# Output weights loaded into the difference buffers, a third PSUM bank for the heads' projections, and another order in the last attention block

## The chip, the cores and the metric

The kernel runs on one core of a Trainium2 chip. The metric is the device time of one execution in microseconds (us). PE is the matmul engine, DVE the vector engine, ACT the scalar (activation) engine, POOL the general-purpose engine, and SP the engine whose queue issues the DMAs here. SBUF is the on-chip working memory, PSUM the eight banks into which PE writes.

## The reference

One decoder layer on 1040 tokens (16 meta tokens and 1024 others) of width 1024. The part that matters here:

```python
a = rmsnorm(h, ln_mix_pre)
proj = a @ w_in
dq, dk, dv, hq, hf, hi, hg = split(proj)
y_diff = diff_attention(dq, dk, dv, ...)     # 4 heads: two softmaxes, p0 - lam * p1, times v, normalised
y_hgrn = hgrn2(hq, hf, hi, hg, ...)          # 4 heads: gated linear recurrence over the tokens
mix = concat([y_diff, y_hgrn]) @ w_out
h = h + rmsnorm(mix, ln_mix_post)
h = h + rmsnorm(conv_ffn(rmsnorm(h, ln_ffn_pre)), ln_ffn_post)
```

## The kernel before, in words

Tokens lie in nine blocks (one of 16 rows, eight of 128) and three groups of blocks, of 272, 384 and 384 columns (`GROUPS`). Matmuls are done on pairs of rounded operands: each value is split into a high and a low part (`split`, ACT makes the high part, DVE or POOL the rest), and three matmuls replace one.

**The order on PE is the program's.** PE follows the text of the program exactly; on the other engines a planner places the instructions by their readiness in its own estimate, except where `issue_after(x)` says that what is traced inside stands behind `x` on x's engine. SP's queue is worked off in the order in which the planner puts its DMAs, and so is every engine: an instruction that waits holds back all behind it.

**interleave (L61)** mixes two kinds of work on PE. `dense` yields projection or output matmuls one by one with a charged cost; the sides are heads, which yield a weight at each point where PE may be given other work. At such a point `fill * weight` units of dense matmuls follow (`FA, FH, FO = 840, 800, 800`). For a projection matmul the charge is `max(115, 0.42 * columns)` (L240), for an output matmul 216.

**Heads.** For each of four heads h, the projections of the HGRN head (hf, hq, hi, hg) run beside attention head h (L916), then those of the next attention head (dq, dk, dv) beside HGRN head h (L919). HGRN head 3 runs beside the first half of the output projection (L1071). `proj_group` (L231) makes one projection for one group of blocks in one PSUM tile from `ps_in`.

**PSUM** has three tags with two buffers each (L146 to L154): "ip" (projections, output sums), "m" (transposes, levels and others) and "S" (two banks per buffer: attention scores, and the HGRN head's output `po`).

**Attention (L624).** For a block, `scores` makes the two score matrices, finds the negative maximum on DVE, and ACT makes the exponentials. The last block has 1040 columns and needs a third bank E, so it has two maxima, and L673 takes the smaller of the two negated ones, `mx`, a DVE instruction on one column; ACT's two exponentials wait for it. At the end DVE combines both softmaxes in `pb` (one instruction over all columns). `values` (L685) transposes `pb` on PE in pieces of four blocks (`pt`) and copies each piece to `at`, in turn on DVE and ACT. `apply` (L710) multiplies by v into `pa`. The order on PE near the end is: scores of block 8 for the second softmax, values of block 7, apply of block 7, values of block 8, apply of block 8.

**HGRN (L413).** `diag`, then seven levels (L445): PE makes small products (`pl`) of the running q and k, then DVE multiplies parts of k (`kr`) and of q (in `mix`) by decays and copies the products to `am`. Each level's products need the multiplies of the level before. Each yields 3 (L503, L506). Level 2 also has POOL make further products of decays. Then three chains (L510), one per group: transposes of k (`pk`, copied to `kn`), `pu`, states `st`, the outputs `po`, their norm `on`, transposes `ss`.

**The difference buffers (L191 to L219).** `wd_sums` loads pieces of the FFN's down weights into five buffers (`wd`) of 256 KB, subtracts them on DVE, and stores the differences; it goes one step per projection group and is done before the last attention head ends. The pool `wdsums` stands on the left side of SBUF, between the activations and the attention pool, and closes with them (L923).

**The output stage (L944 to L1071).** `load_wr(n, k)` loads a 128 x 512 piece of the output weights, half n, k-th of eight, into one of three raw buffers ("wr"); `load_wo` splits it. First half: L1001 splits the mix of the first two blocks and stores the parts (`mix_split`, to `msc`, read back by `mix_load` for the second half), then L1003 loads and splits all eight pieces. `out_first` (L1034) sums the first half block by block; meanwhile two pieces of the second half are loaded ahead (L1045), and each block splits those loaded during the one before (L1047 to L1050).

Of the kernel before, what the change touches and what calls it, by code (L numbers as in the profile page):

```python
# [87 lines left out]
def layer_kernel(ctx: ExitStack, tc: tile.TileContext, x, meta, table, lbl, gpre, gpost, win,  # L88
# [99 lines left out]
        base = start(GROUPS[g][0])  # L188
        return acts[l][g][:, ks, t0 - base:t1 - base]

    ws_cm, wsp = pool("wdsums", 5)  # L191
    wsp.tile([P, 32], F32, tag="lineup_ws", name="lineup_ws", bufs=1)

    last_load = []

# [27 lines left out]

    wd_sums = down_sums()
    at_p_cm, ap_ = pool("attn", 1)
    z_cm, zp = pool("pre", 2, "right")

    def load_m(m, name, where=None, bufs=4):
        return [load_split(win[m][:, 512 * c: 512 * (c + 1)], f"{name}_{c}", where, bufs) for c in range(2)]

    def proj_group(g, parts, name, evac):  # L231
        b0, b1 = GROUPS[g]
        t0, t1 = start(b0), start(b1 - 1) + P
        n = t1 - t0
        pt = ps_in(f"pi_{name}_{g}")
        for k in range(KD):
            yield from proj_step(pt[:, :n], parts, k, t0, t1, lambda: evac(g, b0, b1, t0, t1, pt[:, :n]))

# [174 lines left out]
    def hgrn_head(t, done=None):  # L413
# [89 lines left out]
        yield 3  # L503
        for lev in range(1, 8):
            level(lev)
            yield 3  # L506

        states = {0: None}

# [114 lines left out]
    def attn(h, tens):  # L624
# [4 lines left out]
        def scores(i):  # L629
            r = rows(i)  # L630
            q0 = start(i)
            W = q0 + r
            nm = f"{h}_{i}"
            pb = ap_.tile([P, 2, L], F32, tag="pb", name=f"pb{nm}", bufs=2)
            st = ap_.tile([P, 12], F32, tag="st", name=f"ast{nm}", bufs=3)
            pend[i] = pb
            nearw = min(256, W)
            j0 = P if i == 0 else 256 - nearw

            def qk_mm(dst, m, c0, n):  # L640
                T.matmul(dst, qs[m][:, q0:q0 + P], ks[m][:, c0:c0 + n], start=True, stop=False)
                T.matmul(dst, qs[m][:, q0:q0 + P], kl[m][:, c0:c0 + n], start=False, stop=True)

            nmx, sm, rc = st[:r, 0:2], st[:r, 2:4], st[:r, 4:5]
            if W <= 512:
                S = ps_s(f"S{nm}")
                for m in range(2):
                    qk_mm(S[:, m, :W], m, 0, W)
                near = S[:r, :, W - nearw:W]
                V.tensor_tensor(near, near, rr[:r, j0:j0 + nearw].rearrange("p (o c) -> p o c", o=1).to_broadcast([r, 2, nearw]), op=ALU.add)  # L650
                V.tensor_reduce(nmx, S[:r, :, :W], axis=AX.X, op=ALU.max, negate=True)
                for m in range(2):
                    A.activation(pb[:r, m, :W], S[:r, m, :W], AF.Exp, bias=nmx[:, m:m + 1], accum_out=sm[:, m:m + 1])
            else:
                for m in range(2):
                    S = ps_s(f"S{nm}_{m}")
                    hw = (W if W <= 912 else 528) // 2
                    for p_ in range(2):
                        qk_mm(S[:, p_, :hw], m, p_ * hw, hw)
                    mx = nmx[:, m:m + 1]  # L660
                    if W <= 912:
                        near = S[:r, 1, hw - 256:hw]
                        V.tensor_tensor(near, near, rr[:r], op=ALU.add)
                        V.tensor_reduce(mx, S[:r, :, :hw], axis=AX.XY, op=ALU.max, negate=True)
                        A.activation(pb[:r, m, :W].rearrange("p (a c) -> p a c", a=2), S[:r, :, :hw], AF.Exp, bias=mx, accum_out=sm[:, m:m + 1])
                    else:
                        E = ps_m(f"E{nm}_{m}")
                        qk_mm(E, m, 528, 512)
                        V.tensor_tensor(E[:r, 256:], E[:r, 256:], rr[:r], op=ALU.add)
                        ex = st[:r, 6 + 2 * m:8 + 2 * m]  # L670
                        V.tensor_reduce(ex[:, 0:1], S[:r, :, :hw], axis=AX.XY, op=ALU.max, negate=True)
                        V.tensor_reduce(ex[:, 1:2], E[:r], axis=AX.X, op=ALU.max, negate=True)
                        V.tensor_tensor(mx, ex[:, 0:1], ex[:, 1:2], op=ALU.min)  # L673
                        A.activation(pb[:r, m, :528].rearrange("p (a c) -> p a c", a=2), S[:r, :, :hw], AF.Exp, bias=mx, accum_out=ex[:, 0:1])
                        A.activation(pb[:r, m, 528:W], E[:r], AF.Exp, bias=mx, accum_out=ex[:, 1:2])
                        V.tensor_tensor(sm[:, m:m + 1], ex[:, 0:1], ex[:, 1:2], op=ALU.add)
                    if m == 0:
                        yield 0.7
            V.reciprocal(rc, sm[:, 1:2])
            V.scalar_tensor_tensor(rc, sm[:, 0:1], nlam[:r], rc, ALU.mult, ALU.mult)  # L680
            V.scalar_tensor_tensor(pb[:r, 0, :W], pb[:r, 1, :W], rc, pb[:r, 0, :W], ALU.mult, ALU.add)
            pend["sum", i] = sm[:, 0:1]
            yield 1.3 if W <= 512 else 0.7

        def values(i):  # L685
# [7 lines left out]
            for pi, blks in enumerate(pieces):  # L693
# [8 lines left out]
                    A.copy(az[i % 2][:META, :r], pt[:META, :r])  # L702
                lo = 1 if pi == 0 else 0
                if n0 > lo:
                    (A.copy if pi % 2 else V.tensor_copy)(at[:, lo:n0], pv[:, lo:n0])
                ats.append(at)
                yield 0.8 if i < 4 else 0.6
            pend["ats"] = ats, pieces
# [44 lines left out]
                yield from values(i + 1)  # L753
        carry.append(pend.pop("tail"))

    def dense(tiles, preload=None, side=iter(())):
        parts = preload
        for idx, (m, name, evac) in enumerate(tiles):
            if parts is None:
                parts = load_m(m, name)  # L760
            nxt = load_m(tiles[idx + 1][0], tiles[idx + 1][1]) if idx + 1 < len(tiles) else None
            for g in range(3):
                next(side, None)
                for step, c in enumerate(proj_group(g, parts, name, evac)):
                    if step == 8:
                        flush()
                    yield c
            parts = nxt
# [145 lines left out]
    for h in range(HEADS):  # L914
        t_h, tiles_h = hgrn_in(h)
        interleave(dense(tiles_h, None, wd_sums), [attn(h, t_a)] + carried(), FA, 1500)  # L916
        if h < HEADS - 1:
            t_a, tiles_a = attn_in(h + 1)
            interleave(dense(tiles_a, None, wd_sums), [hgrn_head(t_h)] + carried(), FH, 1500)  # L919

    assert next(wd_sums, wd_sums) is wd_sums
    line_up(hp, 24)
    close(at_p_cm, ws_cm, at_cm)  # L923
    y_cm, yp = pool("y0", 1)
    y0 = yp.tile([P, NBLK, 512], F32, tag="y0", name="y0")
    m0 = yp.tile([P, KD, 36], F32R, tag="m0", name="m0")
# [15 lines left out]
    kept = kpp.tile([P, 2, KD, P], F32R, tag="kept", name="kept")  # L942

    def load_wr(n, k):  # L944
        raw = wp.tile([P, 512], F32, tag="wr", name=f"wor{n}_{k}", bufs=3)
        last_load.append(SY.dma_start(raw, wout[P * k: P * (k + 1), 512 * n: 512 * (n + 1)]))
        return n, k, raw

# [49 lines left out]
                T.matmul(py[:34], m0[:, k, :34], wo[k][l], start=(k == 0 and l == 0), stop=(k == last and l == 1))  # L998
                yield 216

    sps = [mix_split(i, 0, 4) for i in FIRST[:2]]  # L1001
    mix_split(0, 0, 7)
    wo0 = [load_wo(*load_wr(0, k)) for k in range(KD)]  # L1003
    wo = []

    pre_last = {}
# [27 lines left out]
    def out_first():  # L1034
# [5 lines left out]
        for j in range(2):  # L1040
# [1 line left out]
            if j == 0:  # L1042
                sp_ = mix_split(FIRST[2], 0, 4)
            A.copy(y0[:, FIRST[j]], pys[j])
        nxt = [load_wr(1, k) for k in (0, 1)]  # L1045
        for n, i in enumerate(FIRST[2:]):
            for w in nxt:  # L1047
                with tc.issue_after(V.last.ins):
                    wo.append(load_wo(*w))
            nxt = [load_wr(1, k) for k in ((2, 3), (4,), (5,), (6,), (7,), ())[n]]  # L1050
            if n == 3:
                ahead.extend(mix_load(2, c) for c in range(4))
            py = ps_in(f"py0_{i}")
# [706 lines left out]
```

## Time and profile before

| | us |
|---|---|
| median of 3 runs (1303.45 to 1305.43) | 1304.05 |
| the profiled execution | 1303.76 |
| its span, from the first to the last instruction | 1302.0 |
| PE busy | 1270.9 |
| DVE busy | 913.7 |
| ACT busy | 691.4 |
| POOL busy | 408.7 |

The granted clock of PE is 0.999 over the span. The heads take about 66 to 516 us, the output stage about 516 to 660 us, and the FFN the rest. In a timeline's row stand the start and length in us, the engine, the line of the program (L54 is the helper that records all DVE and ACT instructions, so these are told apart by their tiles), the operation, the tile written, `<-` the tiles read, sizes and count; in brackets the idle time of the engine just before it, and what ended it.

### The profile page before, as it was taken

The numbers are of one execution on the slowest core, as the hardware profiler recorded it, in microseconds if no ns is written. First come the engines' busy times: TensorE is split into PE (matmuls) and PEld (weight loads), VectorE is DVE, ScalarE is ACT, GpSimd is POOL, SyncE is SP. The second block draws the span as 40 slices with busy tenths as digits, with TensorE's granted clock in tenths as the row PEclk, the third lists the DMA queues.
The fourth block names the chain that finished last, engine by engine and source line by source line (L and its number), as shares of the span: only waits on it lengthen the run. The fifth ranks groups of instructions, "written<-read, shape, count | busy, mean of one in ns | idle before, by whom it ended". The sixth has DMA issues, their size and how long they took to land.

```text
span 1302.0 us, 26327 instructions
## 1 busy us (share of the span) xinstructions
PE 1270.9 (98%) x10236; PEld 1181.6 (91%) x10236; DVE 913.7 (70%) x1577; ACT 691.4 (53%) x1672; POOL 408.7 (31%) x322
## 2 busy tenths in 40 slices
PE   7999999999999999999999999999999999999997
PEld 6899999999998999777899999999999998888886
DVE  7575656575757565746888787787787787697587
ACT  7465356545653566446665454455455454454454
POOL 3211212021212120013155666766766740010020
PEclk9999999999999999999999999999999999999999
DMA  6221323122322211836711322222222236965363
GB/s 221 93 90 62 100 90 105 54 99 98 98 78 91 77 38 44 268 106 206 260 58 66 106 93 79 74 97 75 74 98 74 74 106 218 333 203 172 94 210 122
DMA packets 84371, 153.07 MB, mean 118 GB/s; under 512 B 9571, under 2 KB 19843, under 8 KB 84246
## 3 DMA queue, kind: packets, MB, share of 16 engines
q1 hardware_dynamic: 84246, 151.39, 35.2%
q8 instruction: 80, 1.31, 0.4%
q14 instruction: 45, 0.37, 0.1%
HBM read 112.69 MB, written 38.67 MB: 116 GB/s over the span
## 4 chain that ended last, share of the span: by engine, by line
PE 87%; DVE 6%; ACT 3%; DMA 2%; issue 1%; SPq 0%; DVEq 0%; ACTq 0%
PE pd L1571 5%; PE pd L1572 5%; PE pd L1570 5%; PE pb L1371 4%; PE pb L1372 4%; PE pb L1373 4%; PE pa L722 3%; PE pa L1372 3%; PE pa L1371 3%; PE pa L1373 3%; PE pc L1371 3%; PE pc L1373 3%; PE pc L1372 3%; PE pq L1350 2%; PE pq L1348 2%; PE pq L1349 2%
## 5 line engine op out<-in xcount | busy, mean ns | idle before, releaser
L1371 PE MATMUL pb<-t,uh 128*128 128x258 f32 (+1 forms) x456 | 127.4, 279 | 0.4 <-DVE u L54 0.4
L1372 PE MATMUL pb<-t,uh 128*128 128x258 f32 (+1 forms) x456 | 127.3, 279 | 0.0
L1373 PE MATMUL pb<-t,ul 128*128 128x258 f32 (+1 forms) x456 | 127.2, 279 | 0.0
L1571 PE MATMUL pd<-wl,gh 128*128 128x512 f32 (+1 forms) x314 | 120.8, 385 | 0.4 <-DVE wl L54 0.3
L1572 PE MATMUL pd<-wh,gl 128*128 128x512 f32 (+1 forms) x314 | 120.8, 385 | 0.0
L1570 PE MATMUL pd<-wh,gh 128*128 128x512 f32 (+1 forms) x314 | 120.7, 384 | 0.0
L54 DVE SCALAR_TENSOR_TENSOR c<-uu,cwt,c 128x512 f32<-128x512 f32 x88 | 94.7, 1077 | 22.3 <-ACT c L54 21.5
L1320 POOL TENSOR_TENSOR c<-c,c 128x512 f32<-128x512 f32 x44 | 64.4, 1463 | 127.2 <-ACT c L54 113.7
L54 DVE SCALAR_TENSOR_TENSOR c<-ug,cwt,c 128x512 f32<-128x512 f32 x88 | 84.0, 955 | 6.6 <-ACT c L54 5.9
L1371 PEld LDWEIGHTS pb<-t,uh 128*128 128x128 f32 x456 | 85.9, 188 | 0.8 <-DVE u L54 0.6
L1372 PEld LDWEIGHTS pb<-t,uh 128*128 128x128 f32 x456 | 85.9, 188 | 0.0
L1373 PEld LDWEIGHTS pb<-t,ul 128*128 128x128 f32 x456 | 85.8, 188 | 0.0
L1372 PE MATMUL pa<-t,uh 128*128 128x256 f32 (+1 forms) x304 | 85.3, 281 | 0.0
L1373 PE MATMUL pa<-t,ul 128*128 128x256 f32 (+1 forms) x304 | 85.2, 280 | 0.0
L1371 PE MATMUL pa<-t,uh 128*128 128x256 f32 (+1 forms) x304 | 85.2, 280 | 0.0
L1373 PE MATMUL pc<-t,ul 128*128 128x256 f32 x304 | 83.9, 276 | 0.0
L1371 PE MATMUL pc<-t,uh 128*128 128x256 f32 x304 | 83.9, 276 | 0.0
L1372 PE MATMUL pc<-t,uh 128*128 128x256 f32 x304 | 83.9, 276 | 0.0
L1571 PEld LDWEIGHTS pd<-wl,gh 128*128 128x128 f32 x314 | 59.0, 188 | 13.7 <-DVE wl L54 1.5
L1572 PEld LDWEIGHTS pd<-wh,gl 128*128 128x128 f32 x314 | 59.0, 188 | 12.0
L1570 PEld LDWEIGHTS pd<-wh,gh 128*128 128x128 f32 x314 | 59.0, 188 | 11.9
L54 ACT ACTIVATE c<-ug,cbt,cwt 128x512 f32<-128x512 f32 x44 | 35.9, 816 | 44.1 <-issue 26.2
(411 smaller groups left out, 4285.7 us busy)
## 6 DMA issues: line engine op xcount, KB each, us to landing
ra<-in_wup_dram SPq DMA_DIRECT2D x76, 256.0 KB, 2.7
wd<-in_wdown_dram SPq DMA_DIRECT2D x44, 256.0 KB, 3.3
tsc<-wd SPq DMA_DIRECT2D x44, 256.0 KB, 2.1
gsc<-c SPq DMA_DIRECT2D x44, 256.0 KB, 2.0
wi<-tsc SPq DMA_DIRECT2D x44, 256.0 KB, 3.0
gi<-gsc SPq DMA_DIRECT2D x33, 256.0 KB, 3.8
wi<-in_wdown_dram SPq DMA_DIRECT2D x33, 256.0 KB, 3.3
msc<-mm SPq DMA_DIRECT2D x21, 256.0 KB, 4.6
```

What stands on the lines that cost most here:

```text
L54: ins = call(*args, **kw)
L722: T.matmul(po[:, :P], w_, vn[:, j], start=(j == 0), stop=(j == i))
L1320: G.tensor_tensor(cg, cg, cu, op=ALU.mult)
L1348: T.matmul(pt, hi[:, s], th[:, k], start=(kh + k == 0), stop=False)
L1349: T.matmul(pt, hi[:, s], tl[:, k], start=False, stop=False)
L1350: T.matmul(pt, lo[:, s], th[:, k], start=False, stop=(kh == 1 and k == 3))
L1371: T.matmul(pt, hi[:, s], th[:, k], start=(first and k == 0), stop=False, skip_group_check=True)
L1372: T.matmul(pt, hi[:, s], tl[:, k], start=False, stop=False, skip_group_check=True)
L1373: T.matmul(pt, lo[:, s], th[:, k], start=False, stop=(k == 3), skip_group_check=True)
L1570: T.matmul(py, gh[:, s], wh, start=(k == 0 and pr not in (3, 7)), stop=False, skip_group_check=True)
L1571: T.matmul(py, gh[:, s], wl, start=False, stop=False, skip_group_check=True)
L1572: T.matmul(py, gl[:, s], wh, start=False, stop=(k == NH - 1), skip_group_check=True)
```

## The change

- The pool of the difference buffers moves to the right side of SBUF and stays open to the end of the first half of the output stage. The raw pieces of the output weights go into its five buffers, except the first three of the first half, which keep the "wr" buffers. All eight loads of the first half are issued ahead of the first two blocks' `mix_split`, and the DMAs of that split stand behind the last of these loads on SP. In `out_first`, four pieces of the second half are loaded at the start in place of two, and each later one a block earlier.
- While an HGRN head runs beside projections, the projection of the third group takes its PSUM tile from "S" in place of "ip".
- After level 2 the HGRN head yields 4 in place of 3.
- In the last attention block the combination of the two softmaxes is cut in two at column 400. The copies of block 7's transposes on DVE stand behind the last `mx` of block 8 (`pend["low"]`) on DVE.
- Two fillers that align addresses (`line_up`) change with the pool.

```diff
@@ down_sums
-    ws_cm, wsp = pool("wdsums", 5)
-    wsp.tile([P, 32], F32, tag="lineup_ws", name="lineup_ws", bufs=1)
+    ws_cm, wsp = pool("wdsums", 5, "right")
...
     at_p_cm, ap_ = pool("attn", 1)
+    line_up(ap_, 32)
...
-    def proj_group(g, parts, name, evac):
+    def proj_group(g, parts, name, evac, wide=False):
...
-        pt = ps_in(f"pi_{name}_{g}")
+        pt = ps_s(f"pi_{name}_{g}")[:, 0] if wide and g == 2 else ps_in(f"pi_{name}_{g}")
@@ hgrn_head
         for lev in range(1, 8):
             level(lev)
-            yield 3
+            yield 4 if lev == 2 else 3
@@ attn
-                        V.tensor_tensor(mx, ex[:, 0:1], ex[:, 1:2], op=ALU.min)
+                        pend["low"] = V.tensor_tensor(mx, ex[:, 0:1], ex[:, 1:2], op=ALU.min)
...
-            V.scalar_tensor_tensor(pb[:r, 0, :W], pb[:r, 1, :W], rc, pb[:r, 0, :W], ALU.mult, ALU.add)
+            for c0, c1 in ((0, W),) if W <= 912 else ((0, start(4)), (start(4), W)):
+                V.scalar_tensor_tensor(pb[:r, 0, c0:c1], pb[:r, 1, c0:c1], rc, pb[:r, 0, c0:c1], ALU.mult, ALU.add)
...
-                    (A.copy if pi % 2 else V.tensor_copy)(at[:, lo:n0], pv[:, lo:n0])
+                    with tc.issue_after(pend["low"].ins) if i == NBLK - 2 else nullcontext():
+                        (A.copy if pi % 2 else V.tensor_copy)(at[:, lo:n0], pv[:, lo:n0])
@@ heads
-            interleave(dense(tiles_a, None, wd_sums), [hgrn_head(t_h)] + carried(), FH, 1500)
+            interleave(dense(tiles_a, None, wd_sums, True), [hgrn_head(t_h)] + carried(), FH, 1500)
...
-    close(at_p_cm, ws_cm, at_cm)
+    close(at_p_cm, at_cm)
@@ output stage
-        raw = wp.tile([P, 512], F32, tag="wr", name=f"wor{n}_{k}", bufs=3)
+        raw = (wp.tile([P, 512], F32, tag="wr", name=f"wor{n}_{k}", bufs=3) if n == 0 and k < 3
+               else wsp.tile([P, 512], F32, tag="wd", name=f"wor{n}_{k}"))
...
-    sps = [mix_split(i, 0, 4) for i in FIRST[:2]]
+    wors = [load_wr(0, k) for k in range(KD)]
+    with tc.issue_after(last_load[-1].ins):
+        sps = [mix_split(i, 0, 4) for i in FIRST[:2]]
     mix_split(0, 0, 7)
-    wo0 = [load_wo(*load_wr(0, k)) for k in range(KD)]
+    wo0 = [load_wo(*w) for w in wors]
...
-        nxt = [load_wr(1, k) for k in (0, 1)]
+        nxt = [load_wr(1, k) for k in range(4)]
         for n, i in enumerate(FIRST[2:]):
-            for w in nxt:
+            for w in [nxt.pop(0) for _ in range((2, 2, 1, 1, 1, 1)[n])]:
                 with tc.issue_after(V.last.ins):
                     wo.append(load_wo(*w))
-            nxt = [load_wr(1, k) for k in ((2, 3), (4,), (5,), (6,), (7,), ())[n]]
+            nxt += [load_wr(1, k) for k in ((4,), (5,), (6,), (7,), (), ())[n]]
...
-    close(w0_cm, ma_cm, h_cm)
+    close(w0_cm, ma_cm, h_cm, ws_cm)
```

More of the change, by code (lines that the diff above doesn't have):

```diff
@@ L754, in attn, with dense @@
         carry.append(pend.pop("tail"))
-    def dense(tiles, preload=None, side=iter(())):
+    def dense(tiles, preload=None, side=iter(()), wide=False):
         parts = preload
@@ L763, in dense @@
                 next(side, None)
-                for step, c in enumerate(proj_group(g, parts, name, evac)):
+                for step, c in enumerate(proj_group(g, parts, name, evac, wide)):
                     if step == 8:
```

## The prediction

> **What bounds the kernel now.** I read the head of the page first, then PE's own list of waits, and only then the timelines around those waits.
>
> ```profile
> span 1302.0 us, 26327 instructions
> ## 1 busy us (share of the span) xinstructions
> PE 1270.9 (98%) x10236; PEld 1181.6 (91%) x10236; DVE 913.7 (70%) x1577; ACT 691.4 (53%) x1672; POOL 408.7 (31%) x322
> ```
>
> PE is busy for 1270.9 of 1302.0 us, so all its idle time together is 31.1 us. The change adds and removes no matmul. It can therefore shorten the kernel only by taking idle time away from PE, and which idle time that is stands in the list of PE's waits (who waited for whom, us in total, times, longest):
>
> ```profile
> PE pt L698 <- DVE at L54: 2.3, 4, 1.0
> PE pg L798 <- DMA grow<-in_gpre_dram: 2.2, 1, 2.2
> PE pl L462 <- DVE mix L54: 2.1, 3, 0.7
> PE pi_dv L243 <- DVE kl L54: 1.9, 3, 0.7
> PE pa L722 <- ACT pb L54: 1.9, 3, 0.8
> PE pk L518 <- DVE kr L54: 1.8, 1, 1.8
> PE py L988 <- ACT woh L54: 1.1, 1, 1.1
> ```
>
> Except for pg, which is the start of the kernel, every line lies in a stage that the change edits. Four edits meet four groups of them: pl (three heads, after level 2), pi_dv (three heads, waiting for a PSUM bank), pa and pt (the last attention block) and pk and py (the output stage). Without pt, which I argue below stays, these are 2.1 + 1.9 + 1.9 + 1.8 + 1.1 = 8.8 us. This is the ceiling of what I count on. The question for each is whether the edit removes the wait, and what is late next.
>
> **Level 2: four shares of filling in place of three.** PE's timeline around the wait in the first head, and at that head's end:
>
> ```profile
> 152.72 0.86 PE L462 MATMUL pl<-mix,kr 128*32 128x16 f32 x48 [0.71 <-DVE mix L54]
> ...
> 188.20 0.39 PE L538 MATMUL po<-st,mix 128*128 128x128 f32 x2
> 188.34 0.42 PE L245 MATMUL pi_dv<-alo,wh_dv 128*128 128x384 f32 x1
> ...
> 189.64 0.34 PE L247 MATMUL pi_dv<-ahi,wl_dv 128*128 128x384 f32 x1
> ```
>
> The level's matmuls stand in PE's fixed order and wait 0.71 us for the multiplies of level 2. The edit places 800 more units of projection ahead of them. A projection matmul with 384 columns is charged 0.42 x 384 = 161 units, so that is 5 matmuls. From 188.34 to 189.64 lie eight of them, seven intervals, 1.30 / 7 = 0.19 us each, so the filling is 5 x 0.19 = 0.9 us and covers 0.71. Nothing is added to PE; the five come from the end of the same list. After the head's last po (188.20) eight projection matmuls are left today and three would be left then, so the list does not run dry. Worth 2.1 us in three heads. The fourth head gets the same filling from output matmuls; no wait on level 2 is listed there, so nothing.
>
> **The third bank for the projections' last group.** The bank that the second dv group needs, and what follows it on PE, then the end of the head:
>
> ```profile
> 172.37 0.48 ACT L54 COPY kn<-pk 128x384 f32<-128x384 f32 x1
> 172.70 1.11 DVE L54 TENSOR_TENSOR kl<-pi_dk,k 64x384 fp32r<-64x384 f32 x2
> 173.96 0.41 PE L243 MATMUL pi_dv<-ahi,wh_dv 128*128 128x384 f32 x1 [0.74 <-DVE kl L54]
> ...
> 190.11 0.56 DVE L54 TENSOR_TENSOR on<-po,nss 128x384 f32<-128x384 f32 x1 [2.21 <-ACT nss L54]
> ...
> 190.49 0.47 ACT L54 COPY vt<-pi_dv 128x384 f32<-128x384 f32 x1
> ...
> 192.02 0.17 PE L641 MATMUL S<-k,q 128*128 128x16 f32 x1
> ```
>
> With two "ip" banks for all groups, the second dv group reuses the bank of the third dk group, which DVE empties until 172.70 + 1.11 = 173.81. With the third groups in "S", it reuses the bank of the second dk group, emptied one evacuation earlier. The wait of 0.74 goes. Next in PE's order are the pu matmuls, which need kn: ready at 172.37 + 0.48 = 172.85, before 173.22, when PE stopped. So nothing else is late at that place: 1.9 us in three heads. The price is on "S", which has two buffers and also serves po and the next head's first scores. While the third dv group holds one, the three po tiles share the other. Each po after the first stands behind the ss transposes of the one before it in PE's order, and these need the same "on" that frees the bank, so no new wait. The next head's scores come at 192.02; the two banks are free at 190.67 (on) and 190.96 (vt). The cover is 1.06 us; if it were gone, every tenth of a microsecond beyond it would cost three tenths in all. I take 0.
>
> **The last attention block.** Rows of the second head; the last one is from the fourth:
>
> ```profile
> 245.68 0.69 DVE L54 TENSOR_REDUCE ast<-E 128x1 f32<-128x512 f32 x1
> ...
> 246.50 1.27 POOL L157 TENSOR_TENSOR wl_dq<-wr_dq,wh_dq 128x512 fp32r<-128x512 f32 x1 [3.47 <-ACT wh_dq L54]
> 246.61 0.56 DVE L54 COPY at<-pt 128x384 f32<-128x384 f32 x1 [0.24 <-ACT az L54]
> 247.09 0.70 DVE L54 TENSOR_TENSOR ast<-ast 128x1 f32<-128x1 f32 x1
> 247.23 0.66 PE L698 MATMUL pt<-ident,pb 128*128 128x128 f32 x4 [0.52 <-DVE at L54]
> ...
> 247.82 0.70 ACT L54 ACTIVATE pb<-S,ast 128x528 f32<-128x528 f32 x1 [0.87 <-DVE ast L54]
> ...
> 249.34 0.49 PE L722 MATMUL pa<-avn,az 128*128 128x128 f32 x2 [0.83 <-ACT pb L54]
> ...
> 500.91 0.15 DVE L54 TENSOR_TENSOR ast<-ast 128x1 f32<-128x1 f32 x1
> ```
>
> DVE copies block 7's transposes (246.61) ahead of the one-column minimum (247.09) on which block 8's exponentials wait. The edit turns the two round: the minimum can start when the reduction ends, at 246.37, in the 0.24 us in which the copy waits for ACT anyway. The exponential then starts up to 0.87 us earlier, more than pa's 0.83 us wait. What is queued behind the new order is the copy, and behind it pt; the copy still starts at about 246.6, so pt's 0.52 stays. I take pa's whole 1.9 and leave pt's 2.3.
>
> The minimum took 0.70 us here and 0.15 in the fourth head. In the slow case POOL's subtraction ran from 246.50 to 247.77, which is where the minimum ended. So the edit pays only if the minimum starts before 246.50, and the margin is 0.13 us. If POOL is first, the minimum ends at 247.77 as now and the copy comes after it: pt then waits until about 248.33, 1.1 us more, of which pa's own wait of 0.83 takes up all but 0.3. That end of this part is 0.3 us lost in each of two heads. By the times of today's rows the minimum is first, and I take that.
> The Trainium skill, "SBUF — State Buffer", section "Who interferes with whom", says that a DVE instruction with two SBUF inputs contends with a GpSimd instruction that reads SBUF, and that issue order decides who blocks. The rows above agree (0.70 against 0.15); by that rule with POOL first the part would be about +0.6 us, and with the minimum first it is the -1.9 of the sum.
>
> Cutting the last block's 1040-column combination in two adds one DVE instruction per head. No pt of that block is among PE's four waits on at in the rows that I looked at, so it gains nothing and costs nothing on the path; its ends are a few tenths either way.
>
> **The output weights.** The core's busy times by stretch (us, PE, PEld, DVE, ACT, POOL, clock, DMA share, GB/s), then the rows of ACT and of SP's queue:
>
> ```profile
> 444.00:516.00 72.00, 70.65 (x491) 68.53 (x490) 42.85 (x100) 44.44 (x133) 10.53 (x9) 1.00 0.11 38
> 516.00:560.00 44.00, 40.53 (x589) 31.20 (x588) 32.77 (x78) 22.06 (x46) 2.34 (x5) 1.00 0.75 241
> ...
> 461.29 40.06 SPq L946 DMA_DIRECT2D wor<-in_wout_dram  x5
> ...
> 525.97 1.93 ACT L54 CAST woh<-wor 128x512 fp32r<-128x512 f32 x3 [2.80 <-DMA wor<-in_wout_dram]
> ...
> 548.30 0.56 SPq L946 DMA_DIRECT2D wor<-in_wout_dram  x1
> ...
> 555.13 0.62 ACT L54 CAST woh<-wor 128x512 fp32r<-128x512 f32 x1 [3.44 <-DMA wor<-in_wout_dram]
> ```
>
> Three buffers let only five of the first half's eight loads go before 516; the last three are issued when the stage has begun, in a stretch with a DMA share of 0.75, and ACT stands 2.80 us for them. PE's py wait of 1.1 follows from this. The edit gives the five later weights the five buffers of the differences, whose work is over by then, and puts all eight loads ahead of the first stores of the split mix on SP. They move into 444 to 516, where the share is 0.11. ACT then finds them landed; the three casts (1.93 us) fit into the 2.80 us in which ACT now stands.
>
> For the second half, the load of 548.30 is cast only at 555.13, 6.8 us later, and ACT stands 3.44 us of it. ACT is in order: a copy and a cast of the mix stand behind it, a DVE subtraction behind those, then the multiply that pk awaits for 1.8 us. The edit issues every such load one block earlier (four at the start, not two, then one per block). A block is 21 output matmuls beside a level, 4 to 5 us; the lead grows by that, more than the 3.44. No wait is added on PE. The stores moved behind the loads on SP are read only in the next stage. Both waits go: 2.9, of which I keep 0.3 back for what ACT may still stand.
>
> **Sum.** 2.1 + 1.9 + 1.9 + 2.9 = 8.8. I subtract 0.3 as said, and 0.35 (half of a 0.71 wait) in each of three heads, since the projections run five matmuls ahead of the levels and DVE's evacuations fall elsewhere: 1.1. This leaves 7.4. The profiled execution took 1303.76 us (span 1302.0 and 1.76 around it): 1296.4. The median shown, 1304.05, is 0.29 above it, so for a median I say 1296.6.
>
> **Rivals.**
> 1. DVE becomes the bound of the levels and the kernel gets slower. After the shift an evacuation like that of 172.70 (1.11 us) could stand ahead of the multiplies of each of levels 4 to 7, in three heads: 4 x 3 x 1.11 = 13.3 us of new waits against 8.8 saved, +4.5, so 1308.6. It decides from 0.7 us per level on. For it: the multiplies of level 2 are late already. Against it: PE lists no wait at levels 4 to 7, and both evacuation and levels keep three shares of filling between them. Chance 0.08.
> 2. The weights stay late. Loads sent earlier draw on the same transfers' capacity and push others back, so the 2.9 stays: 7.4 - 2.6 = 4.8 saved, 1299.2. For it: 0.75 of capacity used from 516 to 560. Against it: five loads leave that stretch for one at 0.11. Chance 0.12. The Trainium skill, "DMA: Bandwidth & Descriptors", section "Issuing engines are not separate DMA queues", says that all DMAs run on the same 16 engines and interleave; by it order alone makes no bandwidth, but it does not deny the move into the idle stretch.
> 3. The heads give nothing: POOL comes before the minimum (+0.6), and what filling and bank save (4.0) returns as waits on the same DVE queue a few matmuls later. Then only the 2.6 of the weights is left: -2.0, 1302.1. For it: pl and pi_dv both wait for DVE, not for PE. Against it: each edit gives PE other work for that time. Chance 0.13.
> 4. More than the ceiling, if pt's 2.3 shrinks too: about 9.7 saved, 1294.3. Chance 0.05.
>
> **How the numbers follow.** The forecast has 0.62. Its own range runs from 5 to 8.8 us saved. The 8-in-10 range leaves out rival 1, most of rival 3 and the last of rival 4: 1293.6 to 1301.6. A change of 0.2%, 2.6 us, is about what a measurement of this kernel can tell from none. Faster by more than that: forecast, rival 2 and rival 4, 0.79; within it: rival 3, 0.13; slower: rival 1, 0.08.
>
> **What would show it.** In the changed profile PE's waits "pl <- mix", "pi_dv <- kl", "pa <- pb", "pk <- kr" and "py <- woh" are gone or below 0.3 us each; "pt <- at" is still about 2; ACT no longer stands for wor; eight wor loads are issued before 516. The level step is wrong if pl waits at a later level, the bank step if S or po waits, the minimum's step if it still takes 0.7 us, the weights' step if ACT's waits for wor stay. The prediction is wrong as a whole if the named waits go and PE's idle time does not fall by about 7 us.

## The result, and the profile after

The changed kernel takes 1296.89 us (median of 6 runs, 1296.41 to 1297.68) against 1303.53 (1303.24 to 1305.43) for the kernel before on the same chip: a ratio of 0.9952 [0.9941, 0.9963], so about 6.3 us faster (7.7 to 4.8); the two medians are 6.6 apart. The profiled execution took 1296.41 us. The head of its page (busy us, share of the span, instructions):

```profile
span 1294.6 us, 26319 instructions
## 1 busy us (share of the span) xinstructions
PE 1269.1 (98%) x10236; PEld 1181.0 (91%) x10236; DVE 916.8 (71%) x1581; ACT 689.2 (53%) x1672; POOL 408.7 (32%) x322
```

The span is 7.4 us shorter. To see where, both traces are cut at two events that they share: the second piece of block 7's transposes in the last attention head (the row `pt`; of the heads' edits, only the end of that block and the fourth HGRN head's filling lie behind it) and the first `pz` near the end of the output stage. The rows of these stretches (length, then busy us of PE, PEld, DVE, ACT, POOL, clock, DMA share, GB/s), before:

```profile
0.00:501.58 501.58, 482.82 (x4391) 458.05 (x4392) 315.70 (x706) 275.17 (x787) 96.34 (x106) 1.00 0.28 91
501.58:580.03 78.45, 74.98 (x813) 61.77 (x814) 46.15 (x113) 37.96 (x105) 2.68 (x6) 1.00 0.46 147
580.03:1302.00 721.97, 713.09 (x5033) 661.77 (x5031) 551.85 (x758) 378.31 (x781) 309.69 (x210) 1.00 0.40 133
```

and after:

```profile
0.00:497.24 497.24, 481.72 (x4392) 457.48 (x4392) 318.29 (x709) 273.26 (x787) 97.45 (x106) 1.00 0.29 94
497.24:572.72 75.48, 74.43 (x814) 62.16 (x815) 45.86 (x114) 37.49 (x105) 2.40 (x6) 1.00 0.42 133
572.72:1294.60 721.88, 712.91 (x5033) 661.34 (x5031) 552.61 (x758) 378.50 (x781) 308.89 (x210) 1.00 0.40 133
```

The heads lost 4.34 us, the output stage 2.97, the rest 0.09. From PE's list of waits after (who waited for whom, us, times, longest; two lines of over 2 us that neither this list nor the prediction's shows, "px <- xs" and "pi_dq <- alo", lie in the first 15 us of the kernel, before and after):

```profile
PE pk L518 <- DVE kr L54: 2.4, 2, 1.2
...
PE pt L699 <- DVE at L54: 2.3, 4, 1.0
...
PE pl L456 <- DVE kr L54: 0.6, 1, 0.6
...
PE pi_dv L243 <- DVE q L54: 0.2, 1, 0.2
PE pl L462 <- DVE mix L54: 0.2, 1, 0.2
```

Of the five waits that were to go, "pl <- mix" is gone from the first three heads (the 0.2 lies in the fourth), and "pi_dv <- kl", "pa <- pb" and "py <- woh" are gone. "pt <- at" stays at 2.3, as the prediction said. "pk <- kr" is different: its 1.8 us of before lay in the output stage and are gone, but the line reads 2.4, in two new places, heads 0 and 2. The one in head 0, with what DVE and POOL do there:

```profile
169.15 1.28 POOL L157 TENSOR_TENSOR wl_hf<-wr_hf,wh_hf 128x512 fp32r<-128x512 f32 x1 [1.39 <-ACT wh_hf L54]
169.22 1.63 DVE L54 TENSOR_TENSOR mix<-mix,tt 128x128 f32<-128x128 f32 x2
170.77 0.68 DVE L54 TENSOR_TENSOR kr<-kr,tt 128x512 f32<-128x512 f32 x1
171.50 0.55 PE L518 MATMUL pk<-ident,kr 128*128 128x128 f32 x3 [1.20 <-DVE kr L54]
```

The same two engines at the same step (level 7 of head 0) in the kernel before:

```profile
169.56 0.28 DVE L54 TENSOR_TENSOR mix<-mix,tt 128x128 f32<-128x128 f32 x1
169.77 0.68 DVE L54 TENSOR_TENSOR kr<-kr,tt 128x512 f32<-128x512 f32 x1
170.37 1.71 DVE L54 TENSOR_TENSOR mix<-mix,tt 128x192 f32<-128x192 f32 x2
170.47 1.39 POOL L157 TENSOR_TENSOR wl_hf<-wr_hf,wh_hf 128x512 fp32r<-128x512 f32 x1 [1.38 <-ACT wh_hf L54]
```

In both, a pair of DVE multiplies lies beside POOL's subtraction and takes over 1.6 us. Before, the long pair stands behind `kr`, and PE does not wait for it. After, POOL starts 1.3 us earlier and DVE's multiplies only 0.3, the planner has put two multiplies ahead of `kr` where there was one, this pair is the long one, and PE waits 1.20 us. DVE shows no idle time there: the loss appears as a longer duration.

The last attention block, second head, after:

```profile
245.68 0.16 DVE L54 TENSOR_TENSOR ast<-ast 128x1 f32<-128x1 f32 x1
245.76 1.27 POOL L157 TENSOR_TENSOR wl_dq<-wr_dq,wh_dq 128x512 fp32r<-128x512 f32 x1 [3.46 <-ACT wh_dq L54]
245.87 0.56 DVE L54 COPY at<-pt 128x384 f32<-128x384 f32 x1
246.12 0.69 ACT L54 ACTIVATE pb<-S,ast 128x528 f32<-128x528 f32 x1
246.49 0.66 PE L699 MATMUL pt<-ident,pb 128*128 128x128 f32 x4 [0.52 <-DVE at L54]
```

The minimum is ahead of POOL by 0.08 us and takes 0.16 in place of 0.70, the exponential no longer waits behind it, and the copy and `pt`'s 0.52 are as they were.

The weights, after: PE's and the others' busy time in the two stretches that the prediction used, then ACT's waits for the raw pieces and, last, the time from issue to landing of all sixteen:

```profile
444.00:516.00 72.00, 70.65 (x479) 68.26 (x478) 45.39 (x104) 46.70 (x137) 8.81 (x8) 1.00 0.17 55
516.00:560.00 44.00, 43.17 (x614) 34.52 (x613) 29.77 (x75) 19.98 (x46) 2.06 (x5) 1.00 0.64 204
```

```profile
ACT woh L54 <- DMA wor<-in_wout_dram: 6.4, 4, 4.5
ACT wh L54 <- DMA wor<-in_wout_dram: 2.9, 1, 2.9
```

```profile
DMA to landing us min/median/max: 2.5/2.9/6.3
```

The DMA share moved as forecast (0.11 to 0.17, and 0.75 to 0.64); before, the median landing took 4.0 us and the longest 6.8. But ACT still stands 9.3 us for these pieces (12.8 before). In this profile it costs PE little rather than being absent: PE's wait that is left behind it is the 0.6 of "pl L456 <- kr".

### The profile page after: what moved, and what is told of

The parts are those of the page before. It is cut to its first block, busy times and chain, and to the rows that moved or that the text cites. A ratio compares the mean times of both kernels' runs of the same rounds, so it can differ in the third digit from the quotient of the medians.

```text
span 1294.6 us, 26319 instructions
## 1 busy us (share of the span) xinstructions
PE 1269.1 (98%) x10236; PEld 1181.0 (91%) x10236; DVE 916.8 (71%) x1581; ACT 689.2 (53%) x1672; POOL 408.7 (32%) x322
## 4 chain that ended last, share of the span: by engine, by line
PE 53%; DVE 2%; ACT 1%; DMA 0%; issue 0%; DVEq 0%; SPq 0%
PE pd L1576 5%; PE pd L1577 5%; PE pd L1575 5%; PE pb L1376 4%; PE pb L1377 4%; PE pb L1378 4%; PE pa L1377 3%; PE pa L1376 3%; PE pa L1378 3%; PE pc L1376 3%; PE pc L1378 3%; PE pc L1377 3%; PE pq L1353 2%; PE pq L1354 2%; PE pq L1355 2%; PE py L991 1%
```

## The experiments

**Each part alone.** Four kernels, on one other chip, each the kernel before with one part of the change. All four expectations first.

The filling alone:

```diff
         for lev in range(1, 8):
             level(lev)
-            yield 3
+            yield 4 if lev == 2 else 3
```

> The kernel before with the filling after level 2 alone (4 in place of 3). Theory (each part takes its own waits away): pl's three waits of 0.7 us go, and with each of them about 0.15 us more, since a matmul's modelled end overlaps the next one's start and hides that much of a stop: 2.6 us faster, span about 1299.4; pi_dv's waits on kl stay at 1.9. Rival (given back at the bank): the projections come five matmuls earlier to the bank that DVE empties no earlier, so that pi_dv's wait grows by up to 0.7 in each of three heads and the gain is under 0.7 us, span above 1301.3.

The third bank alone:

```diff
-    def proj_group(g, parts, name, evac):
+    def proj_group(g, parts, name, evac, wide=False):
...
-        pt = ps_in(f"pi_{name}_{g}")
+        pt = ps_s(f"pi_{name}_{g}")[:, 0] if wide and g == 2 else ps_in(f"pi_{name}_{g}")
...
-            interleave(dense(tiles_a, None, wd_sums), [hgrn_head(t_h)] + carried(), FH, 1500)
+            interleave(dense(tiles_a, None, wd_sums, True), [hgrn_head(t_h)] + carried(), FH, 1500)
```

> The kernel before with the third group's projections in S alone. Theory: pi_dv's three waits on kl (1.9 us) go with about 0.15 us each on top, 2.3 us faster, span about 1299.7; pl's 2.1 stays; no wait of S or po. Rival: what follows (pu, pk, the chains) waits for the same DVE queue, so the gain is under 1 us, span above 1301.0.

The last attention block alone (order and cut):

```diff
-                        V.tensor_tensor(mx, ex[:, 0:1], ex[:, 1:2], op=ALU.min)
+                        pend["low"] = V.tensor_tensor(mx, ex[:, 0:1], ex[:, 1:2], op=ALU.min)
...
-            V.scalar_tensor_tensor(pb[:r, 0, :W], pb[:r, 1, :W], rc, pb[:r, 0, :W], ALU.mult, ALU.add)
+            for c0, c1 in ((0, W),) if W <= 912 else ((0, start(4)), (start(4), W)):
+                V.scalar_tensor_tensor(pb[:r, 0, c0:c1], pb[:r, 1, c0:c1], rc, pb[:r, 0, c0:c1], ALU.mult, ALU.add)
...
-                    (A.copy if pi % 2 else V.tensor_copy)(at[:, lo:n0], pv[:, lo:n0])
+                    with tc.issue_after(pend["low"].ins) if i == NBLK - 2 else nullcontext():
+                        (A.copy if pi % 2 else V.tensor_copy)(at[:, lo:n0], pv[:, lo:n0])
```

> The kernel before with the last attention block's order and its cut combination alone. Theory: pa's three waits on pb (1.9 us) go with about 0.15 us each on top, 2.3 us faster, span about 1299.7; pt on at stays at 2.3, the one-column minimum takes 0.16 us in all heads. Rival: on DVE the copies come later and the block gives back what it wins at pt, under 0.7 us, span above 1301.3.

The weights alone: the changed kernel with the three edits above undone (the parameter `wide` goes too).

```diff
-            yield 4 if lev == 2 else 3
+            yield 3
...
-                        pend["low"] = V.tensor_tensor(mx, ex[:, 0:1], ex[:, 1:2], op=ALU.min)
+                        V.tensor_tensor(mx, ex[:, 0:1], ex[:, 1:2], op=ALU.min)
...
-            for c0, c1 in ((0, W),) if W <= 912 else ((0, start(4)), (start(4), W)):
-                V.scalar_tensor_tensor(pb[:r, 0, c0:c1], pb[:r, 1, c0:c1], rc, pb[:r, 0, c0:c1], ALU.mult, ALU.add)
+            V.scalar_tensor_tensor(pb[:r, 0, :W], pb[:r, 1, :W], rc, pb[:r, 0, :W], ALU.mult, ALU.add)
...
-                    with tc.issue_after(pend["low"].ins) if i == NBLK - 2 else nullcontext():
-                        (A.copy if pi % 2 else V.tensor_copy)(at[:, lo:n0], pv[:, lo:n0])
+                    (A.copy if pi % 2 else V.tensor_copy)(at[:, lo:n0], pv[:, lo:n0])
...
-            interleave(dense(tiles_a, None, wd_sums, True), [hgrn_head(t_h)] + carried(), FH, 1500)
+            interleave(dense(tiles_a, None, wd_sums), [hgrn_head(t_h)] + carried(), FH, 1500)
```

> The kernel before with the output weights in the difference buffers and their order alone. Theory: py on woh (1.1) and pk on kr (1.8) go, with the two small ones beside them (0.2 and 0.3) 3.4 us and 0.15 us on top of each, against new waits in the stage of about 0.8 us: 3.0 us faster, span about 1299.0. Rival (the DMA engines are as full as before, loads moved ahead push the others back): ACT stands for wor as long as before, 12 us, and the gain is under 1 us.

Measured. The second and third columns are times against the kernel before (1302.33 us, same chip); the last two are the lengths of the two stretches of the profiled execution, cut at the same events as above (before: 501.58 and 78.45).

| part alone | median, us | ratio | heads, us | output stage, us |
|---|---|---|---|---|
| filling | 1302.74 | 1.0005 [0.9996, 1.0015] | 501.87 | 76.02 |
| bank | 1298.95 | 0.9977 [0.9968, 0.9987] | 499.14 | 78.72 |
| last block | 1299.60 | 0.9982 [0.9973, 0.9992] | 499.24 | 76.42 |
| weights | 1299.77 | 0.9979 [0.9970, 0.9988] | 501.65 | 73.79 |

The heads' lengths add up: +0.29 - 2.44 - 2.34 + 0.07 = -4.42, and the whole change has -4.34. The output stage varies from one execution to the next without any edit to the weights (the filling acts there too, in the fourth head): 78.45, 76.02 and 76.42, on average 77.0 (the bank's 78.72 is left out, since its granted clock in that stretch was 0.98). With the new weights, here and in the profiles of the kernels below, it lies between 73.79 and 75.76, on average 74.8 (one left out again, with 0.98). Some 2.2 us are therefore gained there, and the ratio of the weights alone says 2.7, but a single profile doesn't give it to better than about 1 us.

The ratios give +0.7, -3.0, -2.3 and -2.7 us, in sum -7.3; the whole has -6.3 (-7.7 to -4.8). The bank, the block and the weights each pay by themselves, by about what was expected (2.3, 2.3 and 3.0), and in each profile the wait that it aims at is gone. For the weights this says less than for the others, since one of their waits also goes without them. The kernel before had 1.8 for "pk <- kr" and 1.1 for "py <- woh" in the output stage. Filling, bank and last block keep the old loads; their lines, in this order:

```profile
PE py L988 <- ACT woh L54: 0.4, 1, 0.4
...
PE py L988 <- ACT woh L54: 1.3, 1, 1.3
PE pk L518 <- DVE kr L54: 1.0, 1, 1.0
...
PE py L990 <- ACT woh L54: 0.6, 1, 0.6
```

The filling's and the last block's profiles have no wait for `kr` in the output stage. Both waits together are thus 2.9, 0.4, 2.3 and 0.6 us in four profiles with the old loads, 1.6 on average, and the prediction took the highest of the four. ACT's standing for the pieces varies too: 8.8 to 12.8 us in these four, 4.4 with the weights alone, and 8.1 to 11.1 in the other profiles with all of the new loads.

The filling gains nothing. In PE's waits of that kernel "pl <- mix" is gone, and these stand there:

```profile
PE pk L518 <- DVE kr L54: 3.1, 3, 1.2
...
PE pi_dv L243 <- DVE kl L54: 0.9, 3, 0.3
```

It removes 2.1 and half of the bank's wait (1.9 to 0.9), and gives 3.1 back at `pk`, in heads 0, 1 and 2 (1.20, 0.73 and 1.20). So the time is that of the expected rival, but its reason is not: the bank's wait did not grow. In its head 0 the rows are those of the changed kernel, POOL first, then the long pair:

```profile
169.36 1.28 POOL L157 TENSOR_TENSOR wl_hf<-wr_hf,wh_hf 128x512 fp32r<-128x512 f32 x1 [1.39 <-ACT wh_hf L54]
169.43 1.63 DVE L54 TENSOR_TENSOR mix<-mix,tt 128x128 f32<-128x128 f32 x2
170.98 0.68 DVE L54 TENSOR_TENSOR kr<-kr,tt 128x512 f32<-128x512 f32 x1
```

So the new wait comes from the filling and not from another part.

**Is it POOL?** The theory is that POOL's subtraction stretches DVE's multiplies. A rival is that DVE is only late with its queue. If the low part of this one piece (the second half of the hf weights) is made by DVE, the collision goes, and DVE's queue gets longer. The changed kernel was also run again, unedited, beside it.

```diff
-    def load_split(src, name, where=None, bufs=4):
+    def load_split(src, name, where=None, bufs=4, eng=None):
...
-        split(hi, lo, raw)
+        split(hi, lo, raw, eng)
...
-        return [load_split(win[m][:, 512 * c: 512 * (c + 1)], f"{name}_{c}", where, bufs) for c in range(2)]
+        return [load_split(win[m][:, 512 * c: 512 * (c + 1)], f"{name}_{c}", where, bufs, V if name[:2] == "hf" and c else None) for c in range(2)]
```

> The changed kernel with the low part of the second half of each hf weight made on DVE in place of POOL. Theory (POOL's subtraction of 1.3 us stretches the multiply ahead of kr at level 7): the pair of multiplies there falls from 1.63 to about 0.6 us, pk's two waits of 1.2 go, 2.7 us faster than the changed kernel, span about 1292. Rival (DVE's queue is late at level 7 by its own work): DVE has 0.69 us more in each head, pk waits at least 0.6 in two heads, gain under 1 us.

> The changed kernel once more, as the yardstick for the runs beside it: span about 1294.6, pk's two waits of 1.2 us on kr as in its first profile.

Measured: 1294.50 us, ratio 0.9940 [0.9925, 0.9955]; the changed kernel beside it 1297.02, 0.9963 [0.9949, 0.9977], with the same 2.4 of "pk <- kr" (the kernel before took 1302.17 on this chip). With DVE in POOL's place `pk` is not on PE's list of waits, and level 7 reads:

```profile
169.40 0.56 DVE L54 TENSOR_TENSOR mix<-mix,tt 128x128 f32<-128x128 f32 x2
169.88 0.69 DVE L54 TENSOR_TENSOR kr<-kr,tt 128x512 f32<-128x512 f32 x1
```

The pair takes 0.56 us in place of 1.63 at nearly the same start and in the same order. DVE has more to do and PE waits less, which refutes the longer queue and supports the collision. The kernel is 2.5 us faster by medians; the 2.4 of `pk` is most of it.

**What is the filling worth inside the change?** The changed kernel with 3 shares again after level 2:

```diff
-            yield 4 if lev == 2 else 3
+            yield 3
```

> The changed kernel with 3 again after level 2. Theory (the filling moves POOL's subtraction onto the multiply ahead of level 7's kr, so that it wins 2.1 at pl and loses 2.4 at pk): pl's three waits of 0.7 come back, pk's two of 1.2 go, within 0.7 us of the changed kernel. Rival (each part takes its own waits away): pl's waits come back and pk's stay, 2.6 us slower than the changed kernel, span about 1297.

Measured: 1295.00 us, ratio 0.9944 [0.9929, 0.9958], 2.0 us below the changed kernel by medians, more than the 0.7 expected. This kernel and the last three below ran on another chip, where the kernel before took 1302.41. All its runs (1294.40 to 1295.81) lie below all of the changed kernel's (1295.93 to 1297.88). The stretch of the heads and, from PE's list, the wait that comes back:

```profile
0.00:496.44 496.44, 480.94 (x4391) 456.91 (x4392) 315.69 (x709) 275.14 (x787) 96.47 (x106) 1.00 0.28 94
```

```profile
PE pl L462 <- DVE mix L54: 2.4, 4, 0.7
```

The heads end 0.80 us earlier than in the changed kernel (497.24), although the three `pl` waits of the heads are back (the fourth, 0.2, lies in the output stage and is in the changed kernel too). By the block 7 event of each head, the filling costs 0.77 in head 0, gains 0.72 in head 1, where the stretched multiply falls behind `kr`, and costs 0.75 in head 2. The remaining 1.2 us lie in the output stage, where one execution against another doesn't decide.

**Cover in place of removal.** If POOL stays as it is, more filling after level 7 should hide the late `kr`; it is taken from the chains that follow.

```diff
-            yield 4 if lev == 2 else 3
+            yield {2: 4, 7: 5}.get(lev, 3)
...
-            yield 2.5
+            yield 2.2
```

> The changed kernel with 5 in place of 3 after level 7 and 2.2 in place of 2.5 in the chains. Theory: 1600 units are 13 matmuls of 272 columns at 0.125 us, 1.7 us of filling ahead of pk, against waits of 1.2: they go, and the projections last to the end, 2.7 us faster than the changed kernel, span about 1292. Rival (the chains live on their filling): pu, po or ss wait for DVE or ACT where 0.24 us less stands between the steps, gain under 1 us.

Measured: 1293.62 us, ratio 0.9936 [0.9921, 0.9951], 3.4 below the changed kernel by medians (2.7 expected); `pk` is off the list. The pair still takes 1.64 us there: the collision is unchanged and now hidden.

**The wait that stays.** `pt` in the last block, with more filling between the two pieces of block 7 and less ahead of block 8:

```diff
-                yield 0.8 if i < 4 else 0.6
+                yield 0.8 if i < 4 else 1.2 if i == NBLK - 2 and pi == 0 else 0.6
...
-                yield 3
+                yield 2.4
```

> The changed kernel with 1.2 in place of 0.6 between the first and the second piece of block 7's transposes, and 2.4 in place of 3 before block 8's. Theory: 0.6 x 840 = 504 units, 4 or 5 matmuls of 272 columns, 0.55 us ahead of the second piece: pt's 2.3 us falls to about 0.5 (what is left of 1.03 in the fourth head), 1.8 us and 0.1 to 0.15 for each of three stops faster, span about 1292.4. Rival (pa behind it takes the wait over): pa on pb comes back, gain under 0.7 us.

Measured: 1295.64 us, ratio 0.9954 [0.9939, 0.9969], 1.4 below the changed kernel by medians, but the runs overlap (1294.84 to 1298.17 against 1295.93 to 1297.88), so the time does not decide. "pt <- at" falls from 2.3 to 0.4, and "pn_vh <- pb" grows from 0.3 to 1.2: by the waits, about half returns.

**The second half's loads.** The changed kernel, but two pieces of the second half at the start and the later ones where they were before:

```diff
-        nxt = [load_wr(1, k) for k in range(4)]
+        nxt = [load_wr(1, k) for k in (0, 1)]
...
-            for w in [nxt.pop(0) for _ in range((2, 2, 1, 1, 1, 1)[n])]:
+            for w in [nxt.pop(0) for _ in range(len(nxt))]:
...
-            nxt += [load_wr(1, k) for k in ((4,), (5,), (6,), (7,), (), ())[n]]
+            nxt += [load_wr(1, k) for k in ((2, 3), (4,), (5,), (6,), (7,), ())[n]]
```

> The changed kernel with the second half's weights loaded as before the change (two at the start, each later one a block later), still into the difference buffers. Theory (the first half's early loads remove py's wait, the loads a block earlier remove pk's in the output stage): pk's wait of 1.8 us on kr in the output stage comes back, 1.8 us slower than the changed kernel, span about 1296.2. Rival (the buffers and the emptier DMA engines do it all): PE's waits stay as in the changed kernel, within 0.5 us of it.

Measured: 1297.65 us, ratio 0.9962 [0.9949, 0.9975]. In time this is not told apart from the changed kernel (0.6 above it by medians), where 1.8 was expected. The waits of its one profile, PE's first, then ACT's:

```profile
PE pl L456 <- DVE kr L54: 1.9, 1, 1.9
```

```profile
ACT woh L54 <- DMA wor<-in_wout_dram: 10.9, 3, 5.5
```

A wait of the size of 1.8 comes back, one step earlier in the head (`pl` and not `pk`), and ACT stands up to 5.5 us for one piece. The nine profiles with the advance have 0 to 0.9 in that place, so this fits the theory. It does not show it: with the old loads, such a wait was 1.8, 0, 1.0 and 0, and this profile's granted clock in that stretch was 0.98.

**The cut of the combination**, undone in the changed kernel:

```diff
-            for c0, c1 in ((0, W),) if W <= 912 else ((0, start(4)), (start(4), W)):
+            for c0, c1 in ((0, W),):
```

> The changed kernel with the last block's combination of the two softmaxes in one instruction again. Theory (no pt of that block waits for it): within 0.3 us of the changed kernel, and no new wait of PE on pb in that block. Rival (the cut lets the block's first transposes begin earlier): pt waits for pb in four heads, 1 us or more slower.

Measured: 1297.65 us, ratio 0.9964 [0.9950, 0.9978], 0.6 above the changed kernel by medians, which these runs can't resolve. No wait for `pb` appears in that block, so the cut covers nothing there. But `pk` waits three times (3.1), once more than in the changed kernel's two profiles: head 1 is added, as in the kernel with the filling alone, which has no cut either. In head 1 POOL's subtraction and `kr` start almost together, first in the changed kernel, then without the cut:

```profile
295.00 1.85 POOL L157 TENSOR_TENSOR wl_hf<-wr_hf,wh_hf 128x512 fp32r<-128x512 f32 x1 [1.91 <-ACT wh_hf L54]
295.02 0.69 DVE L54 TENSOR_TENSOR kr<-kr,tt 128x512 f32<-128x512 f32 x1
...
295.59 1.28 POOL L157 TENSOR_TENSOR wl_hf<-wr_hf,wh_hf 128x512 fp32r<-128x512 f32 x1 [1.91 <-ACT wh_hf L54]
295.62 1.80 DVE L54 TENSOR_TENSOR kr<-kr,tt 128x512 f32<-128x512 f32 x1
```

With the cut POOL is the one that is held up, without it `kr`, and PE waits 0.72 us. How the cut, in another head's block, shifts this by hundredths of a microsecond is not shown.

**Both fillings together** (after level 7 and between the pieces of block 7; the diffs are those above):

> The changed kernel with both the moved filling around level 7 (5 and 2.2) and the moved filling around block 7's transposes (1.2 and 2.4). Theory (two stages, sums add): 3.4 and 1.4 us faster than the changed kernel, about 1292.2 as a median on its chip. Rival: the block's waits only move to pn_vh, nothing beyond the 3.4, about 1293.6.

Measured: 1292.39 us, ratio 0.9925 [0.9910, 0.9939], 1.2 us below the better of the two alone and 4.6 below the changed kernel by medians. The first difference is not resolved, since the runs overlap (1291.74 to 1293.77 against 1293.02 to 1294.38); the second is. What tops PE's list then, apart from the start of the kernel:

```profile
PE pn_vh L358 <- ACT pb L54: 1.2, 4, 0.3
PE py L991 <- DMA mp<-msc: 1.1, 1, 1.1
```

## Why the prediction was right, and where it was not

The forecast was 7.4 us off the span, and the span fell by 7.4; 1296.6 us was said and 1296.89 measured. The mechanism was right for three parts of four. That the total fits so closely is luck: one term failed, others were too small, and the two spans are single executions of kernels whose output stage varies by up to 2.4 us.

**Filling after level 2: the step failed.** The prediction gave it 2.1 us, less a reserve of 0.35 in each of three heads. The wait that it names goes, but alone it gains nothing (1.0005), and inside the change the heads are 0.80 us shorter without it. The prediction looked for the price in DVE's evacuations and did not follow POOL: five matmuls moved forward bring the projections' work forward. ACT's evacuation of a projection, before and with the filling alone:

```profile
165.16 1.93 ACT L54 CAST k<-pi_dk 64x384 fp32r<-64x384 f32 x4
...
164.04 1.94 ACT L54 CAST k<-pi_dk 64x384 fp32r<-64x384 f32 x4
```

Behind it on ACT stand the casts of the hf weight, and behind these POOL's subtractions, so that the second of them also comes 1.1 us earlier (170.47 to 169.36), onto the multiplies ahead of `kr`. The part of rival 3 that says the heads' waits return "a few matmuls later" is what happened to this edit; they return at level 7, and not on DVE's queue alone but through POOL.

**Third bank: right, too small.** "pi_dv <- kl" is gone, no wait of `S` or `po` came, and the two pieces of cover named in the prediction held. 1.9 was forecast; the heads are 2.44 shorter with it alone.

**Last attention block: right, too small.** The minimum was first, though by 0.08 us and not by the 0.13 computed, which is a narrow margin; `pa` no longer waits and `pt` still does. 1.9 was forecast, 2.34 measured in the heads.

**Why bank and block each give some 0.5 more than the listed waits** can be read from the starts of the matmuls. The last one ahead of a stop of `pi_dv` and of one of `pa` in the kernel before (the matmuls behind these stops, at 173.96 and 249.34, stand in the prediction):

```profile
172.93 0.29 PE L247 MATMUL pi_dv<-ahi,wl_dv 128*128 128x272 f32 x1
...
248.22 0.29 PE L245 MATMUL pi_hg<-alo,wh_hg 128*128 128x272 f32 x1
```

Such matmuls start 0.125 us apart where nothing stops them, but are shown as 0.29 long. A listed wait begins at the shown end, so it leaves out some 0.16 us of each stop, as the expectations of the single parts assumed. From start to start, less 0.125 each, the three stops of `pi_dv` are 2.40 us and the three of `pa` 2.41; the heads became 2.44 and 2.34 shorter. The prediction took the listed waits for the whole loss. It also expected PE's idle time to fall by about 7 us, and the page shows 5.6; the other 1.8 are in PE's busy time (1270.9 to 1269.1) at the same number of matmuls. The hidden part of the stops accounts for some of that, but busy time varies by itself: with the weights alone it is 0.8 us less in the heads, where that kernel is as long as the one before.

**Weights: size right in part by luck, one reason wrong.** 2.6 was forecast, 2.7 measured alone (3.9 to 1.6). Early issue into the idle stretch is as described, eight loads go before 516, and PE's two waits go. But the 2.9 behind the forecast was read from one execution, and three others with the old loads had 0.4, 2.3 and 0.6. And "ACT then finds them landed" did not hold: it stands 9.3 us in place of 12.8. ACT's waits for wor, which the prediction named as the sign that this step is wrong, stayed in good part, and PE hardly felt them. Rival 2 is thus half true in its mechanism and wrong in its time.

**Rival 1** (DVE bounds the levels, slower) did not occur: no new wait at levels 4 to 6 of the first three heads, and at level 7 the cost came from POOL, 1.2 us in two heads in place of 13.3 in all. **Rival 4** (pt shrinks too) did not occur by itself; it took an edit of its own.

In sum the terms were +0.29, -2.44, -2.34 and about -2.7 (filling, bank, block, weights): 7.2 off, where 8.8 less 1.4 was written. The reserve was the right size for the wrong reason: the filling alone missed its 2.1 by 2.4 us, and the bank and the block made up for 1.0 of that. What stays open is how the output stage's gain divides between the first half's loads and the second's, and how much of its variation, 2.4 us between executions without the new weights, is the landing of transfers.

## What to carry to other kernels

When filling is put in front of a wait, follow what it pulls forward on every in-order engine, POOL's operations too, up to the next instruction that PE needs; here it removed a wait at level 2 and made one at level 7. Count a stop of PE from start to start, since the listed waits left out 0.16 us of each here, and read a wait behind a DMA from more than one execution. Time each part of a compound change alone: here three parts paid and one did not, and removing that one made the kernel faster. A wait of an engine off the path may stay large without harm, so judge an edit by what PE waits for behind it.

## What the runs showed of the hardware

A DVE operation on two SBUF operands that starts while a POOL subtraction of 128 x 512 (1.28 us) runs lasts until about the end of POOL's operation: a pair of 128 x 128 multiplies took 1.63 us in place of 0.56, and the one-column minimum 0.70 in place of 0.16. It shows as a longer duration, with no idle time and no releaser, so that the list of waits names only the victim's consumer.

Which of the two suffers depends on who starts first, within a tenth of a microsecond. With POOL 0.07 us ahead of the pair (169.15 and 169.22), the pair was stretched from its start and POOL took 1.28. With DVE 0.10 us ahead (170.37 and 170.47, before the change), POOL took 1.39 and the stretch came after. With the minimum 0.08 us ahead, it took its usual 0.16. The Trainium skill, "SBUF — State Buffer", section "Who interferes with whom", says that such a DVE instruction contends with a GpSimd instruction that reads SBUF, and that issue order decides who blocks. These three cases (1.63, 1.39 and 0.16 us) agree with it. At a few hundredths the starts in the trace no longer tell which was first: in head 1 POOL is shown 0.02 us ahead of `kr` and is the one held up (1.85 us, `kr` 0.69), and without the cut 0.03 us ahead, with `kr` held up (1.80 us, POOL 1.28).
